# Decode attention over paged keys and values: one page of all eight batches per step, in place of one page of four

## The chip, the cores and the metric

One core of a Trainium2 chip runs one launch. The metric is the device time of that launch in microseconds (us). The chip's engines have a name each in the profile: PE is TensorE's matmul stream and PEld its weight loads, DVE is VectorE, ACT is ScalarE, POOL is GpSimd, and SP is the engine that issues most of the loads. A DMA issued on an engine's queue waits in that engine's order of instructions.

## What is computed

One layer of a hybrid decoder, for a prompt of 1024 tokens and for 32 sample tokens (8 batches of 4). One input projection feeds four parallel groups of heads (A: gated DeltaNet, B: Mamba-2 SSD, C: forgetting attention, D: cross-attention); their gated outputs go through one output projection and a LayerNorm. The change touches only the part of group C that serves the sample tokens, the decode attention:

```python
fk = cache_fox_k[l][page_table].reshape(bs, past_len, FOX_HEADS, FOX_DH)   # 8 batches, 32 pages of 128 tokens
fv = cache_fox_v[l][page_table].reshape(bs, past_len, FOX_HEADS, FOX_DH)
s = jnp.einsum('bqhd,bkhd->bhqk', q, k) * FOX_DH ** -0.5
s = s + cq[..., :, None] - ck[..., None, :]       # cumulative log-forget gates
p = jax.nn.softmax(jnp.where(k_pos <= q_pos, s, NEG_BIG), axis=-1)
o = jnp.einsum('bhqk,bkhd->bqhd', p, v)
```

So each of the 8 batches reads 32 pages of keys and values, 512 KB a page (128 partitions of 4096 bytes: 512 columns of keys, 512 of values), 256 pages or 134 MB in all.

## The kernel before, in words

Three things run interleaved between about 98 us and 920 us.

The **projections** (`projections`, L1607, and `projections_b`, L1624) are cut into units. A unit that does a third of a projection's columns (`proj_g`, L345) is 24 matmuls of 352 columns on the whole 128x128 array (L356): three products (high and low halves of the weights and of x) for each of 8 slices of the contraction. 117 of the 137 units that `projections` yields are of this kind; the other 20 prepare the chunks of group A (`gdn_chunks`, L930) and are mostly work for VectorE and ScalarE. Another 21 units of the first kind (L1701) stand after the decode in the program and are pulled forward where TensorE has room. A projection's weights come by one 512 KB load on SP's queue into a single staging buffer (L336, L339), and are split by ScalarE (L341) and GpSimd (L342) into two halves with two buffers each. Outputs of the projections pass through "row" tiles (`row_tile`, L325; 4320 bytes per partition). There are 7 of them before the change (`nrow`, L1638). They serve the x rows and the weights of the first 100 us too, then the q, k and v rows, and the convolutions' input and output (L896), where q, k and v of a head stay in three of them until `gdn_chunks` has used them.

The **decode** (`decode`, L644) takes the batches in two groups of four. For each group it goes through 32 pages. A step of 64 gathers the log-forget row (L672, GpSimd), accumulates it (L675, VectorE), loads four pages (`page`, L744, into `npg` = 10 page tiles, on SP's queue), and calls `decode_block` (L710):

- 16 score matmuls (L718), each with 32 stationary columns, so four of them (one per batch) sit side by side in the array; plain float32, recorded as 32 instructions;
- minimum with bias (L722, L725), two exponentials (L726, L727) and the running sum (L729) on VectorE and ScalarE;
- one transpose on TensorE (L732, shown as L219) and a copy to SBUF by ScalarE (L734);
- 4 matmuls with the values (L737), again side by side, 512 columns each, recorded as 8 instructions;
- the scaled accumulation into the group's output (L742, VectorE).

A page tile comes free when the step's value matmuls have read it. PSUM holds one bank for the scores (`dA`), one for the transpose (`dT`) and two for the products (`dO`). After the 64 steps both groups take one more block each against the 32 new tokens (L689), one after the other, and finish (L690 to L707).

The **order**. `weave` (L136) writes the program so that after each of 67 decode steps a share of 115 of the 137 units follows:

```python
weave((self.decode(), 67), (proj, 116 + 3 * NB - NA0))   # L1676: 116 + 9 - 10
run(proj)                                                # L1677: the other 22 units
```

The order of the instructions on each engine is then fixed when the kernel is built (L1789), along a simulated timeline: what stands earlier in the program goes first as soon as its inputs are ready in that simulation, and what stands later fills in. At run time each engine keeps that order. When the decode has ended, its buffers are given to the prompt's forgetting attention (`fox`, L545) and the DeltaNet scan, which begin at 819.9 us in the profile.

Of the kernel before, what the change touches and what calls it, by code (L numbers as in the profile page):

```python
# [22 lines left out]
NS = 32  # L23
# [11 lines left out]
NB = 3  # L35
GL = 2
NBIG = dict(qd=2, QK=2, Kt=2, wv=2, wkT=2)
NA0 = 10
# [132 lines left out]
class K:  # L171
# [472 lines left out]
    def decode(self):  # L644
# [19 lines left out]
        state = []  # L664
        for gr in range(2):
# [3 lines left out]
            st = [None, None, None, dp.tile([128, 512], F32, name=f"Oacc{gr}")]  # L669
            for j in range(32):  # L670
                lf = dp.tile([128, 128], F32, tag="lf", name="lf", bufs=4)
                nc.gpsimd.indirect_dma_start(out=lf, out_offset=None, in_=I["logf"],  # L672
                                             in_offset=bass.IndirectOffsetOnAxis(ap=ix[:, j:j + 1].bitcast(U32), axis=0))
                cb = dp.tile([128, 128], F32, tag="cb", name="cb", bufs=3)
# [10 lines left out]
            nc.vector.scalar_tensor_tensor(out=cb, in0=cn, scalar=last, in1=self.c(f"dnew{gr}"), op0=ALU.add, op1=ALU.add)  # L685
            state.append((st, cb))
# [23 lines left out]
    def decode_block(self, QD, gr, st, cb, n, key, value):  # L710

        nc, dp = self.nc, self.dp
        m, l, _, O_ = st
        ps = self.g("dA")

        for hp in range(4):
            for b in reversed(range(4)):
                nc.tensor.matmul(ps[32 * b:32 * b + 32, 0:n], lhsT=QD[:, 4 * gr + b, hp, :], rhs=key(hp, b),  # L718
                                 start=(hp == 0), stop=(hp == 3), tile_position=(0, 32 * b))
        S = dp.tile([128, 128], F32, tag="dS", name="dS", bufs=3)  # L720
        mb = dp.tile([128, 4], F32, tag="dmb", name="dmb", bufs=6)
        nc.vector.tensor_tensor_reduce(out=S[:, 0:n], in0=ps[:, 0:n], in1=cb, op0=ALU.add, op1=ALU.min, scale=1.0, scalar=3e38,  # L722
                                       accum_out=mb[:, 0:1])
        if m is not None:
            nc.vector.tensor_tensor(out=mb[:, 0:1], in0=mb[:, 0:1], in1=m, op=ALU.min)  # L725
            nc.scalar.activation(out=mb[:, 1:2], in_=m, func=AF.Exp, scale=-1.0, bias=mb[:, 0:1])  # L726
# [1082 lines left out]
```

## Time and profile before

| | |
|---|---|
| median of 3 runs | 1447.03 us (1434.15, 1447.47, 1447.03) |
| the profiled execution | 1434.86 us |
| its span, first to last instruction | 1433.1 us |
| TensorE busy in the span | 1329.7 us (93%) |
| mean granted clock of TensorE | 0.976 |
| decode, first score matmul to the last value matmul on a page | 114.2 to 770.6 us |

A line of a timeline gives start, duration, engine, line, operation, out<-in by the program's names, and shapes; "x32" is the number of instructions merged in it, and a bracket tells how long the engine stood idle before and what ended the wait. TensorE's matmuls are pipelined: the distance from one start to the next is what a matmul costs, not the duration shown. A line of waits gives the total, the number of times and the longest.

### The profile page before, as it was taken

What the parts mean: (1) busy time and instruction counts of PE and PEld (TensorE: products, weight loads), DVE (VectorE), ACT (ScalarE), POOL (GpSimd) and SP (SyncE); (2) the same over time, 40 slices, a digit from 0 to 9 for tenths busy, and PEclk for the clock granted to TensorE, in tenths of its full rate; (3) what the DMA queues carried; (4) which work ended last, traced back from release to release, by engine and by line L of the source; (5) the groups of instructions that cost most, each with busy time, mean ns of one, the idle gap of its engine ahead of it and who ended that gap; (6) DMA issues with size and microseconds to landing.
All of it is one profiled execution on the core that took longest, in us unless ns stands there. A gap on an engine that the chain in (4) does not pass through costs nothing. (4 is left out here: it accounts for less than half of the span.)

```text
span 1433.1 us, 30270 instructions
## 1 busy us (share of the span) xinstructions
PE 1329.7 (93%) x11222; PEld 1110.0 (77%) x11222; DVE 823.8 (57%) x2141; ACT 494.7 (35%) x1280; POOL 442.4 (31%) x465
## 2 busy tenths in 40 slices
PE   7999999999899999999998899898988979999995
PEld 6899888888778877888887878776766756666764
DVE  4523223256576767534245655677676648856588
ACT  4422222233435343322233244454444421213232
POOL 1445322233425444432212100011111026544456
PEclk9999999999999999999999999899999999999998
DMA  6559888978778897888877834657547576655322
GB/s 246 196 169 374 331 299 323 321 269 281 240 284 306 282 307 248 303 287 323 308 259 175 239 91 118 239 147 208 137 129 252 175 234 205 198 160 121 96 67 106
DMA packets 184477, 324.30 MB, mean 226 GB/s; under 512 B 47177, under 2 KB 110954, under 8 KB 184330
## 3 DMA queue, kind: packets, MB, share of 16 engines
q1 hardware_dynamic: 113744, 241.39, 50.4%
q10 hardware_dynamic: 41930, 59.11, 11.6%
q0 software_dynamic: 28656, 21.88, 6.2%
q8 instruction: 88, 1.44, 0.4%
q14 instruction: 59, 0.48, 0.1%
HBM read 262.23 MB, written 60.01 MB: 225 GB/s over the span
## 5 line engine op out<-in xcount | busy, mean ns | idle before, releaser
L356 PE MATMUL pj<-xh,wh 128*128 128x352 f32 x1152 | 382.2, 333 | 13.1 <-ACT wh L341 5.0
L356 PE MATMUL pj<-xh,wl 128*128 128x352 f32 x1152 | 379.5, 329 | 3.3 <-DVE wl L342 3.3
L356 PE MATMUL pj<-xl,wh 128*128 128x352 f32 x1152 | 379.1, 329 | 0.0
L356 PEld LDWEIGHTS pj<-xh,wh 128*128 128x128 f32 x1152 | 219.1, 191 | 28.1 <-issue 10.7
L356 PEld LDWEIGHTS pj<-xh,wl 128*128 128x128 f32 x1152 | 219.8, 191 | 11.5 <-issue 6.3
L356 PEld LDWEIGHTS pj<-xl,wh 128*128 128x128 f32 x1152 | 219.3, 190 | 10.6 <-issue 9.9
L1574 PE MATMUL op<-wo,mh 128*128 128x512 f32 x512 | 162.9, 398 | 3.1 <-DVE lr L1587 1.6
L672 POOL DMA_INDIRECT lf<-in_logf,ix x64 | 67.9, 1062 | 203.4 <-DVE cb L675 163.4
L342 POOL TENSOR_TENSOR wl<-wr,wh 128x1024 fp32r<-128x1024 f32 x41 | 97.9, 2387 | 104.3 <-ACT wh L341 94.3
L742 DVE SCALAR_TENSOR_TENSOR Oacc<-Oacc,dmb,dO 128x512 f32<-128x512 f32 x64 | 47.5, 743 | 142.3 <-PE dO L737 134.1
L1574 PEld LDWEIGHTS op<-wo,mh 128*128 128x128 f32 x512 | 95.6, 190 | 29.6 <-issue 6.0
L1574 PE MATMUL op<-wo,ml 128*128 128x512 f32 x256 | 102.0, 401 | 5.5 <-POOL ml L1546 5.5
L917 DVE SCALAR_TENSOR_TENSOR y<-u,cw,y 128x1080 f32<-128x1080 f32 x54 | 80.1, 1484 | 21.9 <-ACT y L915 21.5
L718 PEld LDWEIGHTS dA<-pg,QD 128*32 128x32 f32 x2048 | 59.8, 109 | 39.7 <-issue 25.8
L718 PE MATMUL dA<-pg,QD 128*32 128x128 f32 x2048 | 80.6, 275 | 7.6 <-DMA pg<-in_cache 7.5
L598 ACT ACTIVATE S<-S,mn 128x512 f32<-128x512 f32 (+2 forms) x96 | 58.5, 610 | 50.8 <-DVE mn L592 24.3
L737 PE MATMUL dO<-pg,dP 128*32 128x512 f32 x512 | 71.8, 605 | 4.1 <-ACT dP L734 3.9
L726 ACT ACTIVATE dmb<-dmb 128x1 f32<-128x1 f32 x64 | 18.7, 293 | 131.6 <-DVE dmb L725 116.3
L1574 PEld LDWEIGHTS op<-wo,ml 128*128 128x128 f32 x256 | 48.4, 189 | 20.2 <-POOL ml L1546 7.1
L592 DVE CUSTOM_DVE_ANT_0 S<-fs,cB 128x512 f32<-128x512 f32 (+2 forms) x96 | 52.5, 551 | 19.9 <-PE ft L219 15.0
L1193 POOL TENSOR_TENSOR rb<-ra,constG 128x4 f32<-128x4 f32 (+1 forms) x9 | 8.7, 971 | 156.5 <-DVE ra L1192 156.5
L620 PE MATMUL fo<-P,vt 128*64 128x128 f32 x576 | 47.9, 288 | 9.6 <-DMA vt<-vD 7.7
(521 smaller groups left out, 2450.2 us busy)
## 6 DMA issues: line engine op xcount, KB each, us to landing
pg<-in_cache SPq DMA_DIRECT2D x256, 512.0 KB
wr<-in_w_in SPq DMA_DIRECT2D x48, 512.0 KB
k<-kD POOLq DMA_DIRECT2D x16, 512.0 KB, 18.2
wq<-in_w_out SPq DMA_DIRECT2D x16, 512.0 KB
mr<-mixD SPq DMA_DIRECT2D x32, 256.0 KB
xr<-in_xT SPq DMA_DIRECT2D x8, 528.0 KB
gateD<-gt ACTq DMA_DIRECT2D x24, 176.0 KB
mrow<-in_w_mem SPq DMA_DIRECT2D x8, 512.0 KB
```

The lines of the kernel that those rows point to most:

```text
L342: (eng or self.se).tensor_tensor(out=l, in0=r, in1=h.bitcast(F32), op=ALU.subtract)
L356: nc.tensor.matmul(ps[:n], lhsT=w[:, k, :], rhs=x[:, k, s], start=(k == 0 and q == 0), stop=(k == KD - 1 and q == 2))
L592: nc.vector.tensor_tensor_reduce(out=S[:, :w], in0=p[:, :w], in1=cB[:, c0:c1], op0=ALU.add, op1=ALU.min, scale=1.0, scalar=3e38, accum_out ...
L598: nc.scalar.activation(out=S[:, :w], in_=S[:, :w], func=AF.Exp, scale=-1.0, bias=mn[:, 0:1], accum_out=rs[:, qt, h2, i:i + 1])
L620: d = nc.tensor.matmul(o[64 * half:64 * half + 64, 0:128], lhsT=vt[:, kt, 64 * h2:64 * h2 + 64], rhs=P[qt, b4], start=(kt == 0), stop=(kt ...
L672: nc.gpsimd.indirect_dma_start(out=lf, out_offset=None, in_=I["logf"], in_offset=bass.IndirectOffsetOnAxis(ap=ix[:, j:j + 1].bitcast(U32), ...
L718: nc.tensor.matmul(ps[32 * b:32 * b + 32, 0:n], lhsT=QD[:, 4 * gr + b, hp, :], rhs=key(hp, b), start=(hp == 0), stop=(hp == 3), tile_posit ...
L726: nc.scalar.activation(out=mb[:, 1:2], in_=m, func=AF.Exp, scale=-1.0, bias=mb[:, 0:1])
L737: nc.tensor.matmul(po[32 * b:32 * b + 32, :], lhsT=P[:n, 32 * b:32 * b + 32], rhs=value(b), start=True, stop=True, tile_position=(0, 32 * b))
L742: nc.vector.scalar_tensor_tensor(out=O_, in0=O_, scalar=mb[:, 1:2], in1=po, op0=ALU.mult, op1=ALU.add)
L917: nc.vector.scalar_tensor_tensor(out=y, in0=u[:, i:i + CWD], scalar=w[:, i:i + 1], in1=y, op0=ALU.mult, op1=ALU.add)
L1574: nc.tensor.matmul(p[:m], lhsT=l[:, k, :], rhs=W[k][0][:, w, s], start=(k == 0 and q == 0), stop=(k == kn - 1 and q == 2))
```

## The change

A step now takes page j of all eight batches. Both groups' log-forget rows are gathered and accumulated, eight pages are loaded, then one `decode_block` does the scores of both groups (32 matmuls, recorded as 64 instructions) into two halves of one PSUM bank, both groups' softmax, two transposes into one bank, one copy of 256 columns, and both groups' value matmuls (16 instructions). There are 32 such steps, and one block for the new tokens of both groups. There are 12 page tiles instead of 10 and 5 row tiles instead of 7; the accumulated rows have 4 buffers instead of 3. `weave` spreads 128 + 9 - 18 = 119 of the 137 units over 35 steps, and 18 units follow.

```diff
-NA0 = 10
+NA0 = 18
...
-        for gr in range(2):
...
-            for j in range(32):
+        for j in range(32):
+            CB, kv = [], []
+            for gr in range(2):
                 lf = dp.tile([128, 128], F32, tag="lf", name="lf", bufs=4)
                 nc.gpsimd.indirect_dma_start(out=lf, out_offset=None, in_=I["logf"],
...
-                cb = dp.tile([128, 128], F32, tag="cb", name="cb", bufs=3)
+                cb = dp.tile([128, 128], F32, tag="cb", name="cb", bufs=4)
...
-                kv = [self.page(gr * 4 + b, j) for b in range(4)]
-                self.decode_block(QD, gr, st, cb, 128, lambda hp, b: kv[b][:, hp * 128:(hp + 1) * 128], lambda b: kv[b][:, 512:1024])
-                yield
-
-            last = dp.tile([128, 1], F32, name=f"last{gr}")
-            nc.vector.tensor_copy(last, st[2])
+                CB.append(cb)
+                kv += [self.page(gr * 4 + b, j) for b in range(4)]
+            self.decode_block(QD, ST, CB, 128, lambda hp, b: kv[b][:, hp * 128:(hp + 1) * 128], lambda b: kv[b][:, 512:1024])
+            yield
...
+        self.decode_block(QD, ST, CB, NS, lambda hp, b: self.ks[:, hp, :], lambda b: self.vs)
         for gr in range(2):
-            st, cb = state[gr]
-            self.decode_block(QD, gr, st, cb, NS, lambda hp, b: self.ks[:, hp, :], lambda b: self.vs)
...
-    def decode_block(self, QD, gr, st, cb, n, key, value):
+    def decode_block(self, QD, ST, CB, n, key, value):
...
+        for gr in (1, 0):
+            for hp in range(4):
+                for b in reversed(range(4)):
+                    nc.tensor.matmul(ps[32 * b:32 * b + 32, 128 * gr:128 * gr + n], lhsT=QD[:, 4 * gr + b, hp, :], rhs=key(hp, 4 * gr + b),
+                                     start=(hp == 0), stop=(hp == 3), tile_position=(0, 32 * b))
         pt = self.g("dT")
...
+        for gr in range(2):
+            st = ST[gr]
+            m, l = st[0], st[1]
...
+            self.tr(pt[:n, 128 * gr:128 * gr + 128], S[:, 0:n])
+            MB.append((m, mb))
+        P = dp.tile([128, 256], F32, tag="dP", name="dP", bufs=2)
+        nc.scalar.copy(P[:n], pt[:n, 0:256])
+        for gr in range(2):
+            po = self.g("dO")
+            for b in range(4):
+                q = 128 * gr + 32 * b
+                nc.tensor.matmul(po[32 * b:32 * b + 32, :], lhsT=P[:n, q:q + 32], rhs=value(4 * gr + b), start=True, stop=True,
+                                 tile_position=(0, 32 * b))
...
-        self.nrow, self.npg, self.nwo, self.nwr, self.nwh = 7, 10, 4, 1, 2
+        self.nrow, self.npg, self.nwo, self.nwr, self.nwh = 5, 12, 4, 1, 2
...
-                    weave((self.decode(), 67), (proj, 116 + 3 * NB - NA0))
+                    weave((self.decode(), 35), (proj, 128 + 3 * NB - NA0))
```

## Rows read from the trace of the kernel before

**Rows 1.** Stretches: length; busy PE, PEld, DVE, ACT, POOL; granted clock, DMA share, GB/s.

```profile
0.00:100.00 100.00, 87.95 (x600) 79.89 (x601) 42.16 (x91) 38.74 (x59) 30.21 (x20) 0.98 0.57 199
100.00:300.00 200.00, 199.14 (x1774) 178.74 (x1776) 66.33 (x167) 50.25 (x134) 69.22 (x59) 1.00 0.90 325
300.00:600.00 300.00, 282.80 (x2513) 242.32 (x2506) 199.92 (x505) 119.60 (x340) 122.81 (x158) 0.98 0.81 277
757.00:820.00 63.00, 54.69 (x376) 48.44 (x369) 40.78 (x90) 19.71 (x37) 11.98 (x20) 0.92 0.76 188
920.00:1100.00 180.00, 158.32 (x1606) 125.16 (x1606) 130.49 (x403) 87.06 (x283) 22.54 (x26) 0.93 0.62 185
```

**Rows 2.** The projections' matmuls alone (L356), by stretch: PE, PEld, clock, DMA share, GB/s.

```profile
98.00:757.00 659.00, 486.09 (x2799) 447.24 (x2797) 0.99 0.85 297
757.00:820.00 63.00, 49.61 (x264) 45.96 (x264) 0.92 0.76 188
820.00:920.00 100.00, 45.33 (x241) 38.89 (x240) 0.98 0.44 134
```

**Rows 3.** PE's waits between 100 and 800 us.

```profile
PE dA L718 <- DMA pg<-in_cache: 7.5, 8, 1.4
...
PE dO L737 <- ACT dP L734: 3.9, 3, 2.6
```

**Rows 4.** PE's timeline: a burst of scores alone, one of products alone.

```profile
114.24 1.08 PE L718 MATMUL dA<-pg,QD 128*32 128x128 f32 x32
115.25 0.43 PE L356 MATMUL pj<-xh,wh 128*128 128x352 f32 x1
...
123.04 1.06 PE L737 MATMUL dO<-pg,dP 128*32 128x512 f32 x8
124.03 0.43 PE L356 MATMUL pj<-xl,wh 128*128 128x352 f32 x1
```

**Rows 5.** PE's timeline, scores of step 11 and products of step 10 joined.

```profile
218.55 0.64 PE L718 MATMUL dA<-pg,QD 128*32 128x128 f32 x16
...
226.84 0.32 PE L356 MATMUL pj<-xh,wl 128*128 128x352 f32 x1
227.00 0.32 PE L356 MATMUL pj<-xl,wh 128*128 128x352 f32 x1
227.25 0.64 PE L718 MATMUL dA<-pg,QD 128*32 128x128 f32 x16
227.71 1.04 PE L737 MATMUL dO<-pg,dP 128*32 128x512 f32 x8
228.57 0.62 PE L718 MATMUL dA<-pg,QD 128*32 128x128 f32 x16
229.12 0.43 PE L356 MATMUL pj<-xh,wh 128*128 128x352 f32 x1
...
235.71 0.94 PE L718 MATMUL dA<-pg,QD 128*32 128x128 f32 x24
```

**Rows 6.** SP's timeline: the four page loads after step 10's products.

```profile
228.78 2.05 SPq L752 DMA_DIRECT2D pg<-in_cache  x4
```

**Rows 7.** SP's waits between 100 and 800 us.

```profile
SPq L752 <- PE dO L737: 115.0, 37, 7.1
SPq L339 <- POOL wl L342: 62.1, 20, 6.3
```

**Rows 8.** DMA from 200 to 300 us: SP's queue (share of 16 engines), issues.

```profile
q1 hardware_dynamic: 7294, 26.57, 75.1%
...
pg<-in_cache SPq DMA_DIRECT2D x44, 512.0 KB
```

**Rows 9.** Groups by tile: count, and duration in ns as minimum, median, maximum.

```profile
L734 ACT COPY dP<-dT x66: 247/265/284, 119.6 to 789.7; 128x128 f32<-128x128 f32 x64, 32x128 f32<-32x128 f32 x2
L722 DVE CUSTOM_DVE_ANT_0 dS<-dA,cb x64: 271/282/292, 115.4 to 759.8; 128x128 f32<-128x128 f32 x64
```

**Rows 10.** PE's timeline at the decode's end.

```profile
769.53 1.06 PE L737 MATMUL dO<-pg,dP 128*32 128x512 f32 x8
...
793.13 1.06 PE L737 MATMUL dO<-vs,dP 32*32 32x512 f32 x8
```

More of the change, by code (lines that the diff above doesn't have):

```diff
@@ L677, in decode @@
                 st[2] = cb[:, 127:128]
[L678 to L683 removed]
+                CB.append(cb)
+                kv += [self.page(gr * 4 + b, j) for b in range(4)]
+            self.decode_block(QD, ST, CB, 128, lambda hp, b: kv[b][:, hp * 128:(hp + 1) * 128], lambda b: kv[b][:, 512:1024])
+            yield
+        CB = []
+        for gr in range(2):
             cb = dp.tile([128, NS], F32, name=f"cnew{gr}")
[L685 to L686 removed]
+            nc.vector.scalar_tensor_tensor(out=cb, in0=cn, scalar=ST[gr][2], in1=self.c(f"dnew{gr}"), op0=ALU.add, op1=ALU.add)
+            CB.append(cb)
+        self.decode_block(QD, ST, CB, NS, lambda hp, b: self.ks[:, hp, :], lambda b: self.vs)
         for gr in range(2):
[L688 to L689 removed]
+            st = ST[gr]
             r1 = dp.tile([128, 1], F32, tag="dr1", name="dr1", bufs=2)
@@ L708, in decode @@
             yield
-    def decode_block(self, QD, gr, st, cb, n, key, value):
+    def decode_block(self, QD, ST, CB, n, key, value):
         nc, dp = self.nc, self.dp
-        m, l, _, O_ = st
         ps = self.g("dA")
[L716 to L726, printed above, removed]
-        nc.scalar.activation(out=S[:, 0:n], in_=S[:, 0:n], func=AF.Exp, scale=-1.0, bias=mb[:, 0:1], accum_out=mb[:, 2:3])
-        if m is not None:
-            nc.vector.scalar_tensor_tensor(out=mb[:, 2:3], in0=l, scalar=mb[:, 1:2], in1=mb[:, 2:3], op0=ALU.mult, op1=ALU.add)
-        st[0], st[1] = mb[:, 0:1], mb[:, 2:3]
-        pt = self.g("dT")
-        self.tr(pt[:n, 0:128], S[:, 0:n])
-        P = dp.tile([128, 128], F32, tag="dP", name="dP", bufs=3)
-        nc.scalar.copy(P[:n], pt[:n, 0:128])
-        po = self.g("dO")
-        for b in range(4):
-            nc.tensor.matmul(po[32 * b:32 * b + 32, :], lhsT=P[:n, 32 * b:32 * b + 32], rhs=value(b), start=True, stop=True,
-                             tile_position=(0, 32 * b))
-        if m is None:
-            nc.vector.tensor_copy(O_, po)
-        else:
-            nc.vector.scalar_tensor_tensor(out=O_, in0=O_, scalar=mb[:, 1:2], in1=po, op0=ALU.mult, op1=ALU.add)
@@ new lines, in decode_block @@
+        P = dp.tile([128, 256], F32, tag="dP", name="dP", bufs=2)
+        nc.scalar.copy(P[:n], pt[:n, 0:256])
+        for gr in range(2):
+            po = self.g("dO")
[3 more added lines that the diff above has]
+                                 tile_position=(0, 32 * b))
+            (m, mb), O_ = MB[gr], ST[gr][3]
+            if m is None:
+                nc.vector.tensor_copy(O_, po)
+            else:
+                nc.vector.scalar_tensor_tensor(out=O_, in0=O_, scalar=mb[:, 1:2], in1=po, op0=ALU.mult, op1=ALU.add)
```

20 lines of the change are left out of this document (17 added, 3 removed).

## The prediction

> **What bounds the kernel now.** I read the stretches first: while the decode runs, TensorE is the busy engine. It is busy 199.1 of 200 us from 100 to 300 us and 282.8 of 300 us from 300 to 600, where VectorE, the next, has 199.9 [rows 1]. The projections' matmuls fill it: 2799 of them between 98 and 757 us, then 264 and 241 more up to 920 us and none later [rows 2]. They start 0.16 us apart (226.84 to 227.00) [rows 5], so the 3304 are 529 us of TensorE's work. The program's own order would have only some 90 units of 24 matmuls done at the 64th decode step (110 of 137 units are written by then, 20 of them without these matmuls), and 2799 are 117: units have been pulled forward, because the decode is the slower of the two interleaved streams. TensorE's order is fixed, so what counts is where a decode burst stands in it and whether its inputs are there.
>
> PE's own waits show that they mostly are: 7.5 us for pages and 3.9 us for the transposed probabilities [rows 3]. DMA is the second scarce thing: 0.90 busy from 100 to 300 us [rows 1], three quarters of the 16 engines for SP's queue, with 44 pages in 100 us [rows 8]. SP's page loads wait 115.0 us for a page tile that the products still read [rows 7]: page tiles, not SP, time the loads.
>
> **The cycle of pages.** Rows 5 and 6 show it. Step 10's scores start at 218.55, its products end at 227.71 + 1.04 = 228.75: 10.2 us. Four loads are issued from 228.78 [rows 6]; with 10 tiles two of them are the last pages of step 12, and step 12's scores start at 235.71, 7.0 us later. Two steps, eight pages: 17.2 us.
>
> **Part 1: bursts joined.** A burst of scores alone takes 114.24 to 115.25 = 1.01 us, one of products alone 0.99 us [rows 4]; joined they take 227.25 to 229.12 = 1.87 us, and entering a burst costs 227.25 - 227.00 - 0.16 = 0.09 us [rows 5]. Joining two saves 0.13 + 0.09 = 0.22 us. PE's timeline enters 92 bursts for the 64 steps (54 times from a projection into scores, 27 into products, 11 from other work): from the first at 114.24 [rows 4] to the last at 769.53 [rows 10]. After, two groups' scores are one burst and their products another: 64, so 28 x 0.22 = **6.2 us less**. Bounds: 0 if the order splits the pairs again, 60 x 0.22 = 13 less if products also join the next step's scores. I take 6.2, since that next step needs pages which these products free.
>
> **Part 2: the chain.** Two copies of 128 columns, 265 ns each [rows 9], become one of 256 (between 0.27 and 0.53 us, not seen before); 64 copies become 32. ScalarE is busy 119.6 of 300 us [rows 1], so these up to 8 us count nothing; uncovered they would add up to 0.27 us to each of 32 chains, 8 us. The two small `last` copies go, also off the path. Gathers, scans, exponentials and accumulations keep their numbers; the scans are pushed past eight page loads of SP instead of four, but run on other queues. With half as many chains I halve the 3.9 us wait for probabilities: **2 us less** (0 to 4).
>
> **Part 3: pages and weights.** With 12 tiles and steps of 8, only four pages can be ahead. The first group's products free four tiles, which take the missing four pages of the next step; the second group's free those for the step after. So the cycle, per eight pages, is: scores to first products, 10.2 us plus the second group's scores (0.9) and its minimum and part of its chain (0.28 us for the minimum [rows 9], about 0.5 in all), 11.6 us; then four pages instead of two. A page costs 75.1 us x 0.524 / 26.57 = 1.5 us of all engines [rows 8], so 7.0 + 3.0 = 10.0 us. Together 21.6 us. Lower end: the 7.0 us already cover four pages and the second chain hides, 17.2. Upper end: two more pages at the 2.27 us at which 44 pages go through 100 us [rows 8], and another us of chain, 24.
>
> What may it be? The pages' steps must end so that the fox stage can start at 820 us as now. From 114.2, with some 25 us for the last block, 32 steps have 681 us: 21.3 us each. The value I take, 21.6, is there within its error, so **0 us**, with more units pulled forward into each step. That uses up the units: the 241 matmuls (39 us) that fill 820 to 920 us [rows 2] are then done before. Fox without filler has TensorE at 158.3 of 180 us, 88% [rows 1]; about 60 us at 12% idle in place of 100 us at 4%: **3 us more** (0 to 10). SP's 512 KB weight loads now stand behind up to eight page loads instead of four; they have a second buffer behind them, and wait 62.1 us for the splitting engine already [rows 7], so 0 (up to 4 x 1.5 = 6 us late, uncovered, about once in a unit group).
>
> A rule of the Trainium skill speaks against this part. Perfetto Trace Analysis, section Optimization Strategy, says that the same gap repeating on the engine that should be saturated can mean too little SBUF for the next tile. The trace of before agrees in kind: the 8 waits for pages [rows 3]. What it would make of this change is the slower rival below.
>
> **Part 4: row tiles, 7 to 5.** TensorE stands 12 us of the first 100 [rows 1], where x and weights pass through them, and 17 us from 300 to 600, where q, k and v hold three. No row shows five tiles. Nothing to gain; at worst as much again as half of these 29 us, 14. The key projections need only two rows at once to free PSUM (the third is filled from SBUF), and a convolution two beside the three held: five suffice, with less lead. I take **3 us more**.
>
> **Part 5: the end.** The last products on a page start at 769.53, the second group's products on the new tokens at 793.13 [rows 10], two chains behind each other. One block does both: some 10 to 14 us earlier. TensorE loses 8.3 us from 757 to 820 and has a clock of 0.92 there [rows 1], 13 us in all; I take **3 us less** (0 to 13).
>
> **Sum.** -6.2 - 2 + 3 + 3 - 3 = -5 us: 1434.9 to 1430 us for the profiled execution. The median of the runs is 12 us above that execution; on it, 1447 becomes **1442 us**. About 1% (14 us) is what a measurement of this kernel can tell from no change, so this is within it.
>
> **Rivals.**
> *Slower: the page cycle.* With four pages ahead, the cycle decides from 21.3 us on. If the order was made for a shorter one, each step's scores wait as the 8 waits do now (7.5 / 8 = 0.94 us): 32 x 0.94 = 30 us. If the order knows it (24 us), units run out: TensorE has, besides 529 us of projections, 64 x 1.9 = 122 us of decode and some 89 us of other work and waits (659 - 448 - 122, up to 757 us), so from 98 they last to 838; by then 30 of 32 steps are done, two follow at 15 us, then the last block, and fox starts near 893, 73 us late with 39 us less to do: +34. Either way about +30 with the gains off: **1477 us** on the median. For it: DMA at 0.90, SP's 115 us. Against: 0.94 us waits are 8 in 64 steps, and SP has DMA time left from 300 us on (0.81). The rule of the Trainium skill quoted above is this case.
>
> *Faster: the waits go as well.* Products also meet the next scores (-7 more), waits for pages and probabilities halve (-4 more), the end gives 8 more: -24, **1423 us**. For it: half as many chains through VectorE where it is busiest. Against: four pages ahead.
>
> *The pair is split.* If the order issues a group's scores when its own four pages are there, there are up to 96 bursts, 4 x 0.22 = 1 us more than now: 1447 + 1 + 3 = 1451 us, no change.
>
> **Chances.** Within 1%: 0.44 (forecast 0.34, split pair 0.10); slower 0.30; faster 0.26. The forecast's own range is 1433 to 1457. For 8 in 10 it must reach into both rivals: 1418 to 1480.
>
> **What would show it.** Right: some 64 entries into bursts on PE; scores of 64 instructions in about 1.9 us; step starts about 21 us apart on average; PE's wait for pages under 10 us; projections' matmuls gone before 860 us; the last products of the new tokens some 10 to 14 us nearer to the last page's. Wrong: a wait for pages on most steps, or step starts 23 us and more apart with PE idle before fox (slower); products and next scores in one burst (faster); idle in the first 100 us over 15 us (row tiles).

## The result, and the profile after

The kernel after takes **1538.86 us** (median of 4 runs, 1533.18 to 1545.44) against 1442.28 us before (4 runs): ratio **1.0677**, 95% interval 1.0601 to 1.0753. It is slower by 6 to 7.5%, outside the forecast's range. The profiled execution took 1545.44 us, its span is 1543.4 us (before 1433.1), so 110.3 us are to be found.

The stretches of [rows 1], in the kernel after (same columns):

```profile
0.00:100.00 100.00, 86.07 (x571) 78.38 (x572) 40.05 (x86) 37.56 (x57) 28.07 (x19) 0.95 0.54 190
100.00:300.00 200.00, 197.95 (x1684) 181.72 (x1683) 53.61 (x154) 48.65 (x117) 70.07 (x59) 1.00 0.79 294
300.00:600.00 300.00, 269.12 (x2279) 241.16 (x2278) 190.18 (x469) 112.92 (x307) 115.75 (x153) 0.95 0.69 241
757.00:820.00 63.00, 56.59 (x458) 48.83 (x457) 32.66 (x65) 20.34 (x45) 7.98 (x9) 1.00 0.74 268
820.00:920.00 100.00, 70.75 (x639) 50.70 (x637) 42.34 (x124) 22.53 (x67) 7.24 (x11) 0.86 0.80 250
920.00:1100.00 180.00, 139.68 (x1423) 106.57 (x1423) 101.62 (x334) 74.32 (x239) 23.43 (x30) 0.88 0.61 158
```

From 100 to 300 us TensorE is as full as before, but the DMA engines do less (0.79 against 0.90): the same busy engine, with fewer pages going through. From 820 on TensorE has holes. What fills it before that are the projections, as in [rows 2] (PE, PEld, clock, DMA share, GB/s):

```profile
98.00:757.00 659.00, 495.53 (x2884) 465.72 (x2884) 0.98 0.73 262
757.00:820.00 63.00, 47.07 (x276) 43.49 (x275) 1.00 0.74 268
820.00:920.00 100.00, 30.74 (x173) 28.41 (x171) 0.86 0.80 250
```

They are ahead of before (2884 against 2799 at 757 us) and are used up at 862 us, while decode still has pages to take. Its end, on PE's timeline:

```profile
868.25 3.14 PE L750 MATMUL dO<-pg,dP 128*32 128x512 f32 x16 [0.46 <-ACT dP L745]
880.32 3.64 PE L724 MATMUL dA<-pg,QD 128*32 128x128 f32 x64 [8.93 <-DMA pg<-in_cache]
...
888.62 1.92 PE L750 MATMUL dO<-pg,dP 128*32 128x512 f32 x16
...
891.33 1.92 PE L750 MATMUL dO<-vs,dP 32*32 32x512 f32 x16
...
918.55 0.58 PE L588 MATMUL fs<-k,q 128*128 128x256 f32 x2
```

Here nothing is left to cover the pages: 8.93 us of idle wait before the last step. Further up the same delay is there but can't be seen on PE. One step, first on PE's timeline, then the page loads between on SP's:

```profile
259.17 1.92 PE L750 MATMUL dO<-pg,dP 128*32 128x512 f32 x16
261.03 0.43 PE L356 MATMUL pj<-xl,wh 128*128 128x352 f32 x1
...
270.66 1.95 PE L724 MATMUL dA<-pg,QD 128*32 128x128 f32 x64
272.55 0.43 PE L356 MATMUL pj<-xh,wl 128*128 128x352 f32 x1
```

```profile
260.25 7.06 SPq L766 DMA_DIRECT2D pg<-in_cache  x8
```

Products end, eight loads go out, and the next scores stand 9.6 us behind the products (261.03 to 270.66), with projections in between. The waits between 100 and 900 us tell it from two sides, PE's and SP's:

```profile
PE dA L724 <- DMA pg<-in_cache: 11.0, 5, 8.9
PE dT L219 <- ACT dS L738: 9.8, 7, 3.5
```

```profile
SPq L766 <- PE dO L750: 161.0, 51, 14.2
SPq L339 <- DMA wr<-in_w_in: 82.7, 12, 10.6
```

PE waits 11.0 us for pages, 8.9 of them in the one wait above. SP waits 161 us for page tiles that the products still read (135.6 of them from 100 to 800 us, the stretch in which before has 115.0 [rows 7]). The fixed order already puts each step's scores where its pages will be there; so a shortage of page tiles shows as **distance between steps**, not as waiting on PE.

By stages, from the first and last starts that the views of single tiles give (the span cut at them). The views of the scores and of fox's products, before and after; the numbers behind the colon are shortest, median and longest duration in ns, then first and last start:

```profile
L718 PE MATMUL dA<-pg,QD x2048: 269/273/298, 114.2 to 757.7; 128*32 128x128 f32 x187
L620 PE MATMUL fo<-P,vt x576: 272/273/476, 826.9 to 1152.5; 128*64 128x128 f32 x192
```

```profile
L724 PE MATMUL dA<-pg,QD x2048: 269/273/423, 129.0 to 883.5; 128*32 128x128 f32 x187
L620 PE MATMUL fo<-P,vt x576: 272/273/476, 935.5 to 1271.1; 128*64 128x128 f32 x192
```

| stage | before | after | difference |
|---|---|---|---|
| up to the first score | 114.2 | 129.0 | +14.8 |
| decode, to the end of the last products on a page | 656.4 | 761.5 | +105.1 |
| from there to fox's first score | 49.3 | 28.0 | -21.3 |
| fox, first score to last product | 332.6 | 352.6 | +20.0 |
| from there to the end | 280.6 | 272.3 | -8.3 |
| span | 1433.1 | 1543.4 | +110.3 |

### The profile page after: what moved, and what is told of

It reads as the page before. It is cut to its first block, busy times and chain, and to the rows that moved or that the text cites. A ratio compares the mean times of both kernels' runs of the same rounds, so it can differ in the third digit from the quotient of the medians.

```text
span 1543.4 us, 30273 instructions
## 1 busy us (share of the span) xinstructions
PE 1357.4 (88%) x11222; PEld 1131.0 (73%) x11222; DVE 808.8 (52%) x2139; ACT 491.2 (32%) x1247; POOL 440.8 (29%) x465
## 4 chain that ended last, share of the span: by engine, by line
PE 33%; DMA 12%; DVE 8%; issue 7%; POOL 3%; ACT 2%; SPq 2%; ACTq 0%; DVEq 0%; POOLq 0%
PE pj L356 11%; PE op L1588 6%; PE dO L750 2%; DMA cmk<-in_cmk 2%; DMA mr<-mixD 2%; DMA cmv<-in_cmv 2%; DMA pg<-in_cache 2%; PE dA L724 1%; PE fo L620 1%; PE ft L219 1%; DMA wr<-in_w_in 1%; DMA A<-aD1A 1%; PE fs L588 1%; DMA bx<-bD 1%; POOL ml L1560 1%
## 5 line engine op out<-in xcount | busy, mean ns | idle before, releaser
L356 PE MATMUL pj<-xh,wh 128*128 128x352 f32 x1152 | 381.2, 332 | 25.6 <-ACT u L214 11.0
L356 PE MATMUL pj<-xh,wl 128*128 128x352 f32 x1152 | 379.0, 329 | 2.1 <-DVE wl L342 2.1
L356 PE MATMUL pj<-xl,wh 128*128 128x352 f32 x1152 | 379.4, 329 | 0.0
L356 PEld LDWEIGHTS pj<-xh,wh 128*128 128x128 f32 x1152 | 219.9, 191 | 37.8 <-ACT u L214 12.1
L356 PEld LDWEIGHTS pj<-xh,wl 128*128 128x128 f32 x1152 | 221.1, 192 | 11.4 <-issue 7.0
L356 PEld LDWEIGHTS pj<-xl,wh 128*128 128x128 f32 x1152 | 220.3, 191 | 9.2 <-issue 8.7
L675 POOL DMA_INDIRECT lf<-in_logf,ix x64 | 63.5, 992 | 196.5 <-DVE dmb L736 172.3
L724 PE MATMUL dA<-pg,QD 128*32 128x128 f32 x2048 | 64.4, 279 | 11.0 <-DMA pg<-in_cache 11.0
L724 PEld LDWEIGHTS dA<-pg,QD 128*32 128x32 f32 x2048 | 55.7, 112 | 18.8 <-issue 15.4
L376 DVE SCALAR_TENSOR_TENSOR gt<-gt,pj 128x352 f32<-128x352 f32 (+1 forms) x48 | 24.3, 505 | 83.3 <-ACT gt L374 81.4
L750 PE MATMUL dO<-pg,dP 128*32 128x512 f32 x512 | 64.3, 621 | 1.0 <-ACT dP L745 0.9
L341 ACT CAST wh<-wr 128x1024 fp32r<-128x1024 f32 x48 | 50.4, 1050 | 36.4 <-DMA wr<-in_w_in 30.4
L374 ACT ACTIVATE gt<-pj 128x352 f32<-128x352 f32 x48 | 22.1, 461 | 116.3 <-PE pj L356 91.7
## 6 DMA issues: line engine op xcount, KB each, us to landing
k<-kD POOLq DMA_DIRECT2D x16, 512.0 KB, 25.6
```

What stands on the lines that cost most here:

```text
L341: nc.scalar.copy(h, r)
L356: nc.tensor.matmul(ps[:n], lhsT=w[:, k, :], rhs=x[:, k, s], start=(k == 0 and q == 0), stop=(k == KD - 1 and q == 2))
L376: nc.vector.scalar_tensor_tensor(out=out, in0=t[:, :m], scalar=1.0, in1=ps[:, :m], op0=ALU.add, op1=ALU.mult)
L724: nc.tensor.matmul(ps[32 * b:32 * b + 32, 128 * gr:128 * gr + n], lhsT=QD[:, 4 * gr + b, hp, :], rhs=key(hp, 4 * gr + b), start=(hp == 0), ...
L750: nc.tensor.matmul(po[32 * b:32 * b + 32, :], lhsT=P[:n, q:q + 32], rhs=value(4 * gr + b), start=True, stop=True, tile_position=(0, 32 * b))
```

## The experiments

The table first, since most readings rest on it. Times are medians, ratios against runs of before on the same chip; the other columns are from the profiled execution: first score on a page, decode from first to last score, fox's first score, how long fox takes, its last product, the projections' last matmul, the first matmul of the output products, the span. All in us.

| kernel | time | ratio (95%) | first score | decode | fox from | fox takes | fox ends | proj. end | output from | span |
|---|---|---|---|---|---|---|---|---|---|---|
| before | | | 114 | 643 | 820 | 333 | 1152 | 916 | 1156 | 1433 |
| after | 1538.9 | 1.068 (1.060 to 1.075) | 129 | 755 | 919 | 353 | 1271 | 862 | 1277 | 1543 |
| 1 before, 5 rows, 12 pages | 1460.5 | 1.018 (1.012 to 1.024) | 119 | 569 | 765 | 364 | 1128 | 940 | 1190 | 1458 |
| 2 after, 13 pages | 1506.7 | 1.050 (1.044 to 1.055) | 133 | 683 | 870 | 347 | 1218 | 945 | 1221 | 1507 |
| 3 short pages, 12 | 1486.3 | 1.036 (1.030 to 1.043) | 125 | 703 | 883 | 314 | 1197 | 942 | 1205 | 1483 |
| 4 short pages, 16 | 1504.7 | 1.049 (1.043 to 1.056) | 125 | 527 | 717 | 416 | 1134 | 984 | 1245 | 1503 |
| 5 page halves | 1678.1 | 1.167 (1.159 to 1.175) | 120 | 692 | 881 | 434 | 1314 | 1157 | 1430 | 1676 |
| 6 as 1, NB 5 | 1435.4 | 0.999 (0.994 to 1.003) | 117 | 586 | 764 | 390 | 1154 | 929 | 1167 | 1441 |
| 7 after, NA0 40 | 1531.7 | 1.065 (1.058 to 1.073) | 127 | 745 | 907 | 350 | 1257 | 852 | 1263 | 1527 |
| 8 after, 10 pages | 1604.8 | 1.120 (1.110 to 1.131) | 127 | 839 | 1025 | 315 | 1339 | 843 | 1342 | 1600 |
| 9 halves, two queues | 1577.8 | 1.094 (1.089 to 1.100) | 127 | 598 | 793 | 439 | 1232 | 1071 | 1344 | 1591 |
| 10 before, 5 rows | 1440.7 | 0.999 (0.995 to 1.003) | 117 | 648 | 823 | 337 | 1160 | 923 | 1164 | 1437 |
| 11 as 1, NB 6 | 1453.4 | 1.010 (1.006 to 1.013) | 117 | 584 | 754 | 400 | 1155 | 923 | 1160 | 1452 |
| 12 before, all units in decode | 1502.8 | 1.045 (1.039 to 1.052) | 114 | 662 | 839 | 355 | 1194 | 863 | 1220 | 1501 |
| 13 after, sample cross behind fox | 1552.3 | 1.078 (1.072 to 1.085) | 130 | 751 | 916 | 296 | 1212 | 860 | 1290 | 1554 |
| 14 after, 4 cross tiles | 1545.8 | 1.075 (1.068 to 1.081) | 126 | 757 | 919 | 358 | 1277 | 861 | 1279 | 1540 |
| 15 as 1, 4 cross tiles | 1447.0 | 1.007 (1.003 to 1.010) | 118 | 572 | 768 | 360 | 1128 | 943 | 1171 | 1445 |
| 16 as 6, 4 cross tiles | 1450.7 | 1.009 (1.005 to 1.013) | 117 | 583 | 760 | 397 | 1157 | 926 | 1161 | 1449 |

### Row tiles or page tiles (1, 10)

The change also cut the row tiles from 7 to 5. Experiment 1 is the old order with the new tiles, 10 the old order with the row tiles alone:

```diff
-        self.nrow, self.npg, self.nwo, self.nwr, self.nwh = 7, 10, 4, 1, 2
+        self.nrow, self.npg, self.nwo, self.nwr, self.nwh = 5, 12, 4, 1, 2   # 1
+        self.nrow, self.npg, self.nwo, self.nwr, self.nwh = 5, 10, 4, 1, 2   # 10
```

> The kernel before (steps of four pages) with 5 row tiles and 12 page tiles. Page-cycle theory: the loss comes from having only four tiles ahead of a step of eight; steps of four with 12 tiles have eight ahead, so this is no slower than before: 1415 to 1450 us, scores not more than 9 us apart where the projections alone run beside them. Row-tile theory: five row tiles hold back units and the first 100 us, so a good part of the 97 us shows here: 1480 us or more.

> The kernel before with 5 row tiles and its 10 page tiles: the row tiles alone. The forecast's term for them was 3 us (0 to 14): total 1435 to 1455. A theory by which they carry the slow-down would have it over 1480. If the first experiment's 1460 us came of the row tiles and not of decode's earlier end, the total here is 1455 to 1470.

The row tiles cost nothing that can be told (0.999). Twelve pages with steps of four shorten decode from 643 to 569 us, where the kernel after, which has the same tiles but steps of eight, takes 755; and fox starts 55 us earlier. Yet the kernel is 1.8% slower than before, where 1415 to 1450 us was expected. Where the early end went is taken up below.

### How many pages lie ahead of a step (2, 8, 3, 4)

The kernel after with 10 and with 13 page tiles, so 2 and 5 ahead of a step of eight instead of 4 (the thirteenth takes the room of a row tile, so there are 4 of those):

```diff
-        self.nrow, self.npg, self.nwo, self.nwr, self.nwh = 5, 12, 4, 1, 2
+        self.nrow, self.npg, self.nwo, self.nwr, self.nwh = 4, 13, 4, 1, 2   # 2
+        self.nrow, self.npg, self.nwo, self.nwr, self.nwh = 5, 10, 4, 1, 2   # 8
```

> The changed kernel with one more page tile and one row tile less (4 and 13). Page-cycle theory: three pages instead of four must come between a step's products and the next step's scores, at about 1.5 us each, 32 steps: 20 to 50 us faster than the changed kernel, 1490 to 1520 us, steps about 21.5 us apart instead of 23. Row-tile theory: fewer rows again, so slower than 1539 us. Theory of the joined block (its longer chain alone): within 10 us of 1539.

> The kernel after with 10 page tiles instead of 12, so 2 ahead of a step of eight instead of 4; all else as it is, the 5 row tiles too. Theory of the page cycle: each step loses the landing of two more pages, some 2 to 4 us, so 32 steps lose 60 to 130 us, fox starts at 970 or later, total 1580 to 1680. Theory of the row tiles (or of the order within a step): no page tile matters, total within 15 us of 1539.

In 3 and 4 a page is 768 of its 1024 columns: the last 256 columns of the values are left out, and the products take columns 256 to 767 in their place, so that 16 tiles have room. 3 keeps 12 of them as the control.

```diff
-  lambda b: kv[b][:, 512:1024])
+  lambda b: kv[b][:, 256:768])
...
-        t = self.dp.tile([128, 1024], F32, tag="pg", name="pg", bufs=self.npg)
+        t = self.dp.tile([128, 768], F32, tag="pg", name="pg", bufs=self.npg)
...
-                                      in_=self.I["cache"][bass.ds(v, 1), :, :]
+                                      in_=self.I["cache"][bass.ds(v, 1), :, 0:768]
```

> The changed kernel with pages cut to 768 of 1024 columns (the last 256 columns of the values are not loaded; the products read columns 256 to 768 of the page in place of the values), same number of matmuls, 12 page tiles. Control for the next run. Page-cycle theory: the four pages to be waited for are a quarter shorter, 4 x 0.4 us a step: steps 1 to 3 us shorter, 1480 to 1525 us. If DMA throughput bounds the decode, a quarter less traffic brings most of the loss back: 1460 us or less.

> The same with pages cut to 768 columns, but 16 page tiles (the same bytes as 12 whole ones), so a whole step can be loaded ahead. Page-cycle theory: the wait for pages between products and next scores goes, steps follow the projections at 17 to 18 us where only projections run beside them, fox starts before 830 us, and the time is at or below that of the kernel before: 1400 to 1450 us. Theory of the joined block or of the row tiles: as the run with 12 short pages, within 15 us.

2, 8 and 3 came in the ranges of the page cycle, and the dose answers. Scores on pages run for 839, 755 and 683 us with 10, 12 and 13 tiles: 84 us for the two tiles taken away, 2.7 us a step, and 72 us for the one added, 2.3 us a step. With 16 short tiles, eight ahead of a step, it is 527 us, against 703 with 12 of the same size. From the tile views, the score matmuls of experiments 8 and 4:

```profile
L724 PE MATMUL dA<-pg,QD x2048: 272/273/423, 127.2 to 966.3; 128*32 128x128 f32 x187
```

```profile
L724 PE MATMUL dA<-pg,QD x2048: 270/273/423, 124.9 to 651.4; 128*32 128x128 f32 x187
```

The matmul has the same median of 273 ns; the distance differs. SP's wait for page tiles follows less clearly: 200.1 us in experiment 8 (100 to 1000 us), 161.0 in the kernel after, 158.5 in experiment 2. The step of both groups is not slow in itself.

The averages hide two stretches. While the chunks of group A are prepared, steps are longer. In the kernel after, nine steps lie between these two starts:

```profile
338.73 1.96 PE L724 MATMUL dA<-pg,QD 128*32 128x128 f32 x64
...
597.19 2.17 PE L724 MATMUL dA<-pg,QD 128*32 128x128 f32 x64
```

They take 28.7 us each, the other 22 take 22.4. From step starts read in the same way, per eight pages, in the chunks' stretch and outside it: 22.1 and 19.3 us before, 18.7 and 17.4 in experiment 1, 25.6 and 21.1 in 3, 17.2 and 16.7 in 4. So the shortage costs most in that stretch, and with a whole step loaded ahead the stretch hardly matters. Which part of the chunks' work lengthens the steps was not tested.

But the total of 4 missed its expectation (1400 to 1450): the last scores came 177 us earlier than in 3, and the kernel's end 18 us later.

### Pages in halves (5, 9)

With all data, a page as a key tile, free at the scores, and a value tile:

```diff
+            kk = [self.page(b, j, 0) for b in range(8)]
+            vv = [self.page(b, j, 1) for b in range(8)]
+            self.decode_block(QD, ST, CB, 128, lambda hp, b: kk[b][:, hp * 128:(hp + 1) * 128], lambda b: vv[b])
...
+        t = self.dp.tile([128, 512], F32, tag="pg" + "kv"[half], name="pg" + "kv"[half], bufs=self.npg)
...
+            v = (nc.scalar if half else nc.sync).value_load(...)      # 9; in 5 nc.sync for both
+        pages.append((nc.scalar if half else nc.sync).dma_start(...))
```

> The kernel after, with each page in two tiles of half the size, one with its keys and one with its values (12 of each, the same bytes, twice the page transfers): a key tile comes free at the scores instead of at the products with the values, some 11 us earlier. Theory of the page cycle: steps shorten from a median of 23 us to 17 to 20 us, fox's first score comes at 740 to 830 instead of 919. Rival, the two groups' scores and products in one step are themselves what is slow (one accumulator, one chain of minimum, exponent and transpose for eight batches): steps stay at 21 us or more, fox starts after 880. For the total there is a second theory, of two chains that end the kernel: decode to fox, and the projections that decode left over to the cross attention of the samples; the output products start when the later one is done (in the kernels run so far 240 to 276 us after the projections' last matmul, or at fox's end) and the kernel ends 258 to 286 us after that. By it the projections' last matmul comes at 930 to 970, the output starts at 1185 to 1225 and the total is 1450 to 1500. If an early decode were worth its time in full, the total would be under 1430.

> As the kernel with page halves (1678 us: there 16 page transfers of a step, each some 1.15 us of SP's queue with its page number, let one load of weights through in 20 to 28 us), but the value halves are issued by ScalarE, so that SP has 8 page transfers a step again. Theory of the page cycle: steps of 17 to 20 us, fox's first score at 740 to 850; the projections' last matmul at 930 to 980, output from 1185 to 1240, total 1450 to 1500. Rival, a step that takes both groups together is itself slow: steps of 21 us or more, fox from 880 on, total 1530 or more. Second rival, ScalarE's own queue: 256 issues with their page numbers at some 0.7 us are 180 us of ScalarE, the evacuations come late and the projections end after 1000, total over 1520 although decode is done early.

Experiment 5 missed (steps of 692 / 31 = 22.3 us, total 1678) for a reason that the expectation had not: SP's queue, shown here on its timeline.

```profile
400.01 9.68 SPq L767 DMA_DIRECT2D pgk<-in_cache  x7
410.55 9.66 SPq L767 DMA_DIRECT2D pgv<-in_cache  x8
420.31 0.44 SPq L339 DMA_DIRECT2D wr<-in_w_in  x1
421.62 12.42 SPq L767 DMA_DIRECT2D pgk<-in_cache  x8
435.07 5.20 SPq L767 DMA_DIRECT2D pgv<-in_cache  x5
```

Eight half pages take 9.7 us here, 1.2 us each, page number included, so SP does little else, and few loads of weights pass. From 100 to 800 us SP waits 13.4 us for the products (135.6 in the kernel after), and ScalarE 90.7 us for loads of weights (29.7):

```profile
SPq L767 <- PE dO L751: 13.4, 9, 6.2
```

```profile
ACT wh L341 <- DMA wr<-in_w_in: 90.7, 19, 8.9
```

At 757 us 1971 of the projections' matmuls are done instead of 2884, and the last of them moves to 1157 us. With the values on ScalarE's queue (9), decode runs in 598 us: with full data too, steps average 598 / 31 = 19 us once key tiles come free early, as the page theory had it. Its projections ended later (1071) than that theory expected, and the total is over its range: both came as the second rival, ScalarE's own queue, had them. The trace agrees with it in kind. From 100 to 800 us ScalarE waits only 8.8 us for loads of weights, but 127.5 us of its idle time are put down to loads of value pages, which stand in its own queue; the largest of these waits:

```profile
ACT dmb L738 <- DMA pgv<-in_cache: 30.5, 6, 7.6
```

Whether this alone sets the projections' end was not tested.

### Units held back (7)

```diff
-NA0 = 18
+NA0 = 40
```

> The kernel after with 97 of the projections' units woven into decode instead of 119 (NA0 40 instead of 18), so that 22 more run behind decode's last page. Theory of the page cycle: decode's step is set by its pages, so fox's first score comes little earlier, at 870 to 910 instead of 919; the projections' last matmul moves from 862 to 920 to 970, the output starts within 30 us of 1277, total 1510 to 1545. Rival, decode is crowded out by the units woven into it: 22 units are some 90 us of TensorE less, fox starts before 850 and ends before 1220, total under 1500.

Decode loses 10 us (755 to 745), and the total came as the page theory had it. But the projections did not end later (852): the order pulls the units forward again, and 3320 of their matmuls stand between 98 and 872 us, against 3329 in the kernel after. So this experiment took nothing out of decode's stretch and does not test whether decode is crowded out. The page tiles do: in 2 the step is shorter with the same units written into it.

### Two chains to the output (6, 11, 15, 16)

In 1, 4, 5 and 9, where decode ends early or the projections late, fox ends 62 to 116 us before the output starts. The output products need the sample tokens' cross attention too, which stands behind the projections in the program: there, output starts 251 to 273 us after the projections' last matmul. PE's timeline in experiment 1 shows it: the transpose that ends the cross attention and, 0.8 us later, the first output product:

```profile
1189.60 0.42 PE L219 MATMUL zot<-constG,xon 128*128 128x128 f32 x1
1190.40 2.06 PE L1531 MATMUL op<-wq,ms 128*32 128x512 f32 x12 [0.38 <-DVE ms L893]
```

Where fox ends last (before, after, 2, 3, 7, 8, 10), it starts 3 to 8 us after fox. So the output starts at the later of **two chains**, decode to fox and projections to cross attention; in the kernel before they meet (the cross attention's last transpose 1146, fox's end 1152, output 1156). To fox belongs the DeltaNet scan that runs beside it: in 12 the output starts 25 us behind fox, right behind the scan's last transposes.

```profile
1218.97 1.11 PE L219 MATMUL sot<-constG,wv 128*128 128x128 f32 x4 [2.31 <-DVE wv L1180]
1220.01 1.94 PE L1531 MATMUL op<-wq,ms 128*32 128x512 f32 x8
```

The rule was read from before, after and 1 to 4; 5 and 9 agreed with it (273 us both), and 6 and 15 were made to test it. 6 takes two more late projections into decode's stretch, 11 three; 15 and 16 give the cross attention's loads four tiles instead of two:

```diff
-NB = 3
+NB = 5          # 6 and 16; 6 in experiment 11
...
-            mk = dm.tile([128, 4, 256], F32, tag="cmk", name="cmk", bufs=2)
+            mk = dm.tile([128, 4, 256], F32, tag="cmk", name="cmk", bufs=4)     # 15, 16
...
-            mv = dm.tile([128, 2, 512], F32, tag="cmk", name="cmv", bufs=2)
+            mv = dm.tile([128, 2, 512], F32, tag="cmk", name="cmv", bufs=4)     # 15, 16
```

> The kernel before with 5 row tiles and 12 pages, as in the first experiment (1460 us, fox's end at 1128, output products from 1190), and two more of the late projections taken into the stretch of decode (NB 5 instead of 3; their weights no longer wait for fox's rows). Theory of two chains: the chain over the projections bounds the output there, so the projections' last matmul comes 10 to 30 us earlier than 940, the output starts at 1150 to 1175 and the total is 1420 to 1445. Rival, the order of the transfers in the sample stages is what costs, whatever the projections do: the output starts at 1185 or later, total 1455 or more.

> The first experiment's kernel (before with 5 rows and 12 pages, 1460 us; fox's end at 1128, output from 1190) with four tiles for the sample cross attention's loads. Two chains: there the chain over the projections ended last, and its last part is this cross attention, 51 us from its last key product to the output; with loads earlier the output starts 10 to 40 us earlier, 1150 to 1180, total 1425 to 1450. If the transfers' bandwidth sets it (share of the DMA engines 0.81 there), nothing changes: output from 1185, total 1452 or more.

> The kernel before with 5 row tiles, 12 pages and three more of the late projections in decode's stretch (NB 6; with NB 5 it was 1435 us, fox's end 1154, output from 1167). Theory of two chains: they end within 10 us of each other here, fox's end at 1155 to 1170, output from 1158 to 1175, total 1425 to 1440, which can't be told from before or is up to 1% faster.

> The same with two more of the late projections in decode's stretch (NB 5, as in the kernel that took 1435 us, fox's end 1154, output from 1167). Fox's end bounds the output there, so the four tiles give at most 13 us: output at 1155 to 1165, total 1420 to 1435. If the extra tiles only pull transfers into fox's stage, fox ends 5 us or more later and the total is 1435 to 1450.

6 and 15 came as the two chains had it: output from 1167 and 1171 instead of 1190, total 25 and 14 us less than in 1. (The second chain has no fixed length: from the projections' last matmul it is 238 us in 6 and 228 in 15.) In 11 and 16 the output starts where expected (1160, 1161), but it then takes 292 and 289 us where before took 277, and the totals, 1453 and 1451, missed. The granted clock behind that start is 0.94 and 0.93 there, 0.97 before and 0.96 in 6; what lowers it, and whether that is all, stays open. None of the four beats before; 6 equals it.

What an exposed second chain looks like, in the stretches of experiment 1 (columns of [rows 1]):

```profile
1120.00:1140.00 20.00, 11.37 (x117) 5.50 (x117) 5.84 (x15) 1.63 (x4) 2.57 (x6) 0.84 0.80 250
1140.00:1160.00 20.00, 5.11 (x41) 2.81 (x41) 4.55 (x28) 1.50 (x3) 1.65 (x3) 0.50 0.77 199
1160.00:1180.00 20.00, 12.56 (x117) 8.45 (x117) 8.62 (x22) 3.47 (x6) 8.58 (x9) 0.50 0.97 328
1180.00:1200.00 20.00, 15.94 (x117) 9.11 (x113) 9.72 (x33) 5.11 (x11) 8.86 (x12) 0.67 0.82 285
1200.00:1220.00 20.00, 20.00 (x89) 15.62 (x89) 13.56 (x35) 5.10 (x11) 7.87 (x10) 0.87 0.56 165
```

Fox ends at 1128; then TensorE has 5 of 20 us of work while the DMA engines are busy, and its clock falls to the lower level.

### Fox without the projections (12, 13, 14)

All of the projections into decode's stretch, in the kernel before, so that fox runs without them as it does after:

```diff
-NB = 3
+NB = 10
...
-NA0 = 10
+NA0 = 0
```

> The kernel before with all the projections woven into decode (NB 10, NA0 0), so that fox's stage runs without them as it does in the kernel after; pages and rows as before. Some 430 more matmuls of the projections come ahead of decode's end, some 65 us, so fox's first score is at 860 to 900. If fox's stage is bound by its own chain (what the kernel after seems to show: 353 us without them against 332 us with them), it takes 320 us or more, ends after 1190, and the total is 1465 to 1510. If the work that is gone from it shortens it, as the forecast had it (3 us lost), it takes 260 to 290 us, ends at 1130 to 1175 and the total is 1425 to 1455.

Fox starts 20 us later (its first 24 us still have projections beside it) and its stage is 355 us: longer by 22 us, like the kernel after's, not shorter. (The expectation's start was too late: most units were pulled forward in the kernel before already.) The numbers came as the branch of fox's own chain had them; experiment 13 shows below that this reading does not hold. The stage as a whole, in the kernels before, after and 12:

```profile
820.00:1152.00 332.00, 302.82 (x3130) 243.28 (x3130) 218.68 (x711) 152.19 (x475) 33.90 (x44) 0.96 0.56 171
```

```profile
919.00:1271.00 352.00, 292.92 (x3083) 219.65 (x3082) 222.55 (x768) 137.95 (x442) 45.97 (x51) 0.89 0.56 156
```

```profile
839.00:1195.00 356.00, 302.54 (x3093) 235.55 (x3094) 213.16 (x731) 146.55 (x462) 38.87 (x50) 0.90 0.60 163
```

TensorE is busy 293 to 303 us in all three, with nearly as many matmuls: what the projections leave is taken by other work. The sample tokens' cross attention, which stands behind fox in the program, lies in the stage in all three (195 matmuls). Behind it in the program stand the sample tokens' parts of groups A and B: 6 of their matmuls lie in before's stage, 249 in the kernel after's, 107 in 12's. With the earlier place in the stage come waits for the cross attention's loads, 26 us in the kernel after where before had 1.1 (PE's waits, 920 to 1271 us):

```profile
PE zs L880 <- DMA cmk<-in_cmk: 16.9, 3, 10.2
PE zo L901 <- DMA cmv<-in_cmv: 9.1, 3, 7.3
```

In 12 the longer waits are others: 11.1 us for fox's keys, 13.0 for the prompt's cross attention. Experiment 13 takes the sample tokens' work out of the kernel after's stage, 14 gives its loads four tiles (the diff of 15) so that they can start earlier:

```diff
                                                      rhs=P[qt, b4], start=(kt == 0), stop=(kt == qt), tile_position=(0, 64 * half))
+                                self.fox_last = d
...
+                with self.tc.issue_after(self.fox_last.ins):
+                    nc.tensor.matmul(ps[32 * h:32 * h + 32, 0:256], lhsT=QM[:, b, h, :], rhs=mk[:, h, :], ...)
```

> The kernel after, with the sample tokens' cross attention (its score matmuls, L880, and so all that follows them) held behind the last product of fox on TensorE. In the kernel after TensorE stands in fox's stage 26 us before loads of that cross attention (16.9 for keys, 9.1 for values); the stage takes 353 us there, 333 in the kernel before. If these waits lengthen it, the stage takes 315 to 335 us and fox ends at 1235 to 1255; the cross attention then lies bare behind it, the output starts 50 to 100 us after fox's end, total 1545 to 1610. If fox's own chain sets the stage, it stays at 345 us or more, fox's end at 1262 or later, total 1575 or more.

> The kernel after with four tiles instead of two for the sample cross attention's keys and values, so that their loads start earlier. If the waits for these loads lengthen fox's stage, they fall from 26 us to under 10 and the stage to 325 to 340 us, total 1515 to 1532. If fox's own chain sets it, the stage stays within 5 us of 353 and the total within 10 us of 1539.

Without the cross attention and what follows it the stage takes 296 us, 56 less, a larger step than was expected (315 to 335 us); from the tile views of 13, fox's scores and products:

```profile
L588 PE MATMUL fs<-k,q x96: 279/475/796, 915.9 to 1201.6; 128*128 128x512 f32 x48, 128*128 128x256 f32 x32, 128*128 128x384 f32 x16
...
L620 PE MATMUL fo<-P,vt x576: 272/273/476, 933.4 to 1212.3; 128*64 128x128 f32 x192
```

So fox's own chain does not hold the stage at 350 us; the work pulled into it does. It is paid for afterwards: in 13 the output starts 77 us behind fox, and the total is 1552 us. In 14 the two waits are 15.5 and 7.2 us, hardly less, and the stage 358: more tiles do not help, so whether it is these waits or the work itself that lengthens the stage remains open.

## Why the prediction was wrong

**The step that failed is Part 3, the cycle of pages.** It took 21.6 us a step between bounds of 17.2 and 24, set beside it a break-point of 21.3 us, and concluded 0 us, "within its error". The term was mis-sized. Measured, the 32 steps start from 129.0 to 880.3 us, 751.3 / 31 = 24.2 us a step, just past the upper bound. Over the break-point that is (24.24 - 21.3) x 31 = 91 us, most of the 99 us by which fox came late; the rest is 14.8 us more at the start, less 8 behind the last step's start (38.2 us to fox, where the break-point had 21.3 + 25).

The working was taken from one pair of steps at 218 us, in the quiet stretch before the chunks of group A. For that stretch 21.6 was near: 22.4 came outside the chunks, and the four pages that a step waits for took 9.6 us (261.03 to 270.66) of the 10.0 that it gave them. The nine steps among the chunks were missing from it: 28.7 us each, 67 of the 91 us. The base shows the same: 17.2 us was that pair, and the kernel before needs 643.5 / 31.5 = 20.4 us per eight pages on average. What the change adds, 21.6 - 17.2 = 4.4 us in the working and 3.8 measured, agrees by luck, as it is 3.1 outside the chunks and 6.7 among them. And of two numbers 0.3 us apart, with bounds of 17 to 24 and 32 steps, "no cost" was the one reading that the bounds did not support: the break-point lay between them.

**The second step that failed is "3 us more" for fox without units.** It took the 39 us of projections out of the stage and scaled the rest with TensorE's share. Measured: +20.0 us. The order fills the room with the next work in the program (experiments 12 and 13), so the 39 us were never "less to do" within the stage.

**The slower rival had the mechanism, the end of the filler and nearly the place** (24 us a step, units out at 838, fox at 893; measured 24.2, 862, 918.5). It was priced at +34 because it credited those 39 us; without the credit its 73 us alone give 1447 + 73 = 1520, and 1538.86 came.

The signs named beforehand: 63 entries into decode bursts on PE (91 before, counted the same way; forecast 64); scores of 64 instructions from 270.66 to 272.55, 1.89 us (forecast 1.9); PE's waits for pages 11.0 us (forecast under 10, and 8.9 of them came after the filler's end); projections gone at 862 (forecast before 860). Steps 23 us and more apart with PE idle before fox was the sign written down for "wrong", and it came: the median step is 23.2 us.

**Part 1** was right in what it counted, and worth nothing: 28 entries of 0.22 us are 6 us of TensorE's time in a stage that the pages set. Experiment 1 enters decode bursts 114 times and has the shorter decode.

**Part 2**: the joined copy takes 373 ns, between its bounds:

```profile
L745 ACT COPY dP<-dT x33: 352/373/380, 138.2 to 890.9; 128x256 f32<-128x256 f32 x32, 32x256 f32<-32x256 f32 x1
```

But PE's wait on the chain did not halve. It moved one link up, to the transposes waiting for the exponentials: 9.8 us, where before had 1.2 there and 3.9 for the copy [rows 3].

**Part 4** was right: rows alone 0.999 (0.995 to 1.003), and 13.9 us of idle time in the first 100. **Part 5** was right in sign and too small: the products on the new tokens start 2.7 us behind the last page's (888.62 to 891.33), 23.6 before, and fox follows 21.3 us sooner, not 3. **Left out** was the start, +14.8 us: SP's first page load goes out at 106.99 us instead of 102.57, and the first step needs eight of them instead of four. Experiment 10, with the row tiles alone, has its first score at 117.5 us, so some 3 us of the 14.8 go with those. The rest was not tested by itself.

The rule of the Trainium skill that the prediction quoted (Perfetto Trace Analysis, section Optimization Strategy: consistent gaps on the engine that should be saturated can mean too little SBUF for the next tile) named the cause. Its sign did not appear: the gap shows once on PE (8.93 us), as other work fills all the earlier ones; what shows the shortage is the step's length, which 10, 12 and 13 tiles move, and less clearly SP's wait for tiles.

## What to carry to other kernels

Where the order is fixed when the kernel is built, a shortage of tiles doesn't show as waiting: measure the distance between steps, over all of them and not in one quiet stretch, compare it with the distance at which the next stage starts on time, and if that lies inside your bounds, price the upper half by the number of steps. Enlarging a step at a nearly fixed number of tiles takes away what can be loaded ahead: here 12 tiles are eight ahead of a step of four, but four ahead of a step of eight. Before paying for a shorter stage, look for the second chain: with two that meet, shortening one alone gave nothing here.

## What the runs showed of the hardware

- In experiment 1 the granted clock fell with TensorE's work and came back late: 0.84 in the 20 us with 11.37 us of work, 0.50 (1.2 GHz) in the next with 5.11, still 0.50 in the next with 12.56, then 0.67 with 15.94 and 0.87 with TensorE full. In these rows an idle spell costs beyond its end. In the kernel after, fox's stage had 0.89 against 0.96.
- A page load cost SP's queue the same for half the bytes. One issue has a median of 333 ns for pages of 512 KB (the kernel after) and for halves of 256 KB (experiment 5); with page numbers, eight halves took 9.66 us, eight whole ones 7.06 us. Twice as many loads of half the size held up the weights' loads on that queue (ScalarE waited 90.7 us for them, 29.7 in the kernel after).

```profile
L766 SPq DMA_DIRECT2D pg<-in_cache x256: 332/333/1854, 107.0 to 871.9; - x128
```

```profile
L767 SPq DMA_DIRECT2D pgv<-in_cache x256: 3/333/842, 115.2 to 812.5; - x128
```
